# Three steps of an attention pipeline change places: the scaling of probabilities, the compressed branch's exponentials, and the compressed branch's PSUM banks

## The chip, the cores and the metric

The kernel runs on one core of one Trainium2 chip. The metric is device time in microseconds (us) of one execution. The kernel before has a median of 1531.22 us over 3 runs (1530.23 to 1532.88).

The engines are called as the profile calls them: PE (TensorE, matrix products), PEld (its weight loads), DVE (VectorE), ACT (ScalarE), POOL (GpSimd) and SP (SyncE, which issues DMAs). Each works through its own list of instructions in order and waits on semaphores for the others.

## The reference, cut to what matters

One decoder layer over 512 positions of width 2048, all in float32. A normalised input is projected to everything that the layer needs. Mixer A is the attention that this change touches; mixer B is a gated spatial mixer; both are projected up, merged by gates, projected out and added to the residual.

```python
h = rms_norm(x, norm_g[l])
proj = h @ w_in[l]
q, kv, g_logits, z_a, uv, z_b, merge_logits = jnp.split(proj, SPLIT_IDX, axis=-1)
o_a = nsa_attention(q, k_c, v_c, k_s, v_s, k_w, v_w, g_logits, ...) * jax.nn.silu(z_a)
o_b = spatial_gating(uv, ln_v_g[l], ln_v_b[l], sgu_w[l], sgu_b[l]) * jax.nn.silu(z_b)
merged = g_a * (o_a @ w_up_a[l]) + g_b * (o_b @ w_up_b[l])
x = x + merged @ w_out[l]
x = x + jax.nn.sigmoid(x @ w_ple_gate[l]) * (p[l] @ w_ple[l])
return rms_norm(x, final_g)
```

The attention has 16 heads in 4 groups of 4, and three branches with keys and values of their own: compressed (31 pooled keys), selected (blocks chosen by the compressed scores) and window. Each branch is a causal softmax with a linear position penalty per head, times a sigmoid gate:

```python
p_c = jax.nn.softmax(sc, axis=-1) * vc_mask
o_c = jnp.einsum('bgrqn,bngd->bqgrd', p_c.astype(vc.dtype), vc)
p_s = jax.nn.softmax(ss..., axis=-1)
p_w = jax.nn.softmax(sw, axis=-1)
o = gate_0 * o_c + gate_1 * o_s + gate_2 * o_w
```

With 512 positions there are 8 blocks and room for 16, so the selected branch takes every causal block, and the window of 512 takes every causal key. Both are therefore full causal attention, with different keys and values.

## The kernel before, in words

**The products.** Each large product is built from three matmuls in a fast float32 form: operands are cut into a high part (cast on ACT, `high`, line 162) and the remainder (subtraction on DVE, `low`, line 168), and high·high, high·low and low·high are added up in PSUM. A generator `gemm()` yields after each small step of these products, and `fill(n)` takes n steps. For the projections `q` and `za` a step is three matmuls of 128x512 (lines 451 to 453). So weight products can be put between any two other pieces of work on PE. `flush()` runs the list `deferred`, in which a step leaves what it wants issued later, often the `low` of a cast just made.

**The attention stage.** It is a pipeline over 48 slots. A head pair `ft` (8 of them, two per group) has six slots, `j` from 0 to 5: a tile `i` of 128 queries, with one of the two long branches or both. Slots 0 and 1 are the two branches of tile 3 (512 keys each), slots 2 and 3 those of tile 2 (384 keys), slot 4 has both branches of tile 1 (256 keys each), slot 5 both of tile 0 (128 each). The loop of line 1592 goes over slots `s` and 3 more steps, builds a list `events`, and runs it. That list is the order of the work, since every engine's list is filled in the order of the calls:

- `front(s)` first transposes the probabilities of slot s-2 on PE (`transpose_probs`, line 1440, tile `ps_t`; the casts to `pth` follow on ACT, the remainders `ptl` are deferred to DVE), then calls `finish`, which also runs `flush()`, then computes the scores of slot s on PE (`scores`, line 1383, tile `ps_s`) and on DVE adds the position penalty and takes the row's extreme in one instruction per row block (line 1389, tiles `prob` and `st`).
- `weigh(s-1)` takes the reciprocal of the sums (line 1409) and scales the probabilities of the slot before by it and by the gate (line 1414), on DVE.
- `exponentials(s)` runs the exponentials of slot s on ACT (line 1398), with their sums.
- `values(s-3, ...)` multiplies the transposed probabilities with the values on PE (lines 1472 and 1473, tile `ps_o`); at the end of a tile `fold` adds up on ACT and DVE (lines 1486 to 1491).
- The compressed branch runs once per group, spread over slots: `cmp_scores` (two halves in the last slot of an odd `ft`, line 1510), `cmp_softmax` (even `ft`, slot 1: transposes on PE, copy on ACT, then `shift` deferred to DVE, lines 1538 to 1540, which itself defers `exps` to ACT, line 1535), `cmp_weigh` (slot 3, DVE and POOL), `cmp_transpose` (slot 4, lines 1558 and 1560) and `cmp_values` (slot 5 of an even `ft`, slot 3 of an odd one, line 1570).

Between events the loop fills in weight products, so many steps per slot that the projections `q` and `za` are spread over the whole stage. An event in `off_pe` has no PE work: it is neither preceded by `flush()` nor followed by a fill.

**The banks.** PSUM is handed out in kinds of two banks each. Kind `s` serves `ps_s` (both banks, one per head) and `ps_c`, the compressed branch's bank, in turn; kind `t` serves `ps_t` (both banks). Whoever wants a bank again waits until its last reader is done: for `ps_s` that is line 1389 on DVE, for `ps_c` a copy on ACT, for `ps_t` the `ptl` remainders on DVE.

Of the kernel before, what the change touches and what calls it, by code (L numbers as in the profile page):

```python
# [16 lines left out]
AF = mybir.ActivationFunctionType  # L17
# [62 lines left out]
def kernel(ctx: ExitStack, tc: tile.TileContext, x, p, norm_g, w_in,  # L80
                      pe_k, w1_k, w2_k, pe_v, w1_v, w2_v, ln_g, ln_b, sgu_w, sgu_b,
                      w_up_a, w_up_b, w_out, w_ple, w_ple_gate, final_g, out):
    nc = tc.nc
# [68 lines left out]
    deferred = []  # L152
# [347 lines left out]
    def finish(name):  # L500
        while name not in done:
            next(run)
        flush()
# [729 lines left out]
    with tc.tile_pool(name="cmp", bufs=1) as cmp:  # L1233
# [76 lines left out]
        c = cmp.tile([P, 1], F32, name="hid_c")  # L1310
# [137 lines left out]
    def front(s):  # L1448
        if 2 <= s <= n_slots + 1:
            transpose_probs(s - 2)  # L1450
        if s < n_slots:
            ft, i, br = slots[s]
            finish(f"q{ft}")
            if i == 3 and br[0] == 0 and ft:
                fill(1)
                lent.append(1)
            scores(s)
# [67 lines left out]
    def cmp_softmax(g):  # L1525
# [7 lines left out]
        def exps():  # L1533
            for r in range(4):
                nc.scalar.activation(c[:, :, r], c[:, :, r], AF.Exp, scale=SLOPE[4 * g + r])

        def shift():
# [4 lines left out]
            deferred.append(exps)  # L1542
        deferred.append(shift)
        pct_t["c"] = (c, st)

# [29 lines left out]
    off_pe = (cmp_keys, cmp_weigh, weigh, exponentials)  # L1575
# [18 lines left out]
    for s in range(n + 3):  # L1594
# [5 lines left out]
        if s < n:  # L1600
            ft, j = slots[s][0], s % 6
        if s < n + 2:
            events.append((front, s))
        if 1 <= s <= n:
            events.append((weigh, s - 1))
        if s < n and ft % 2 == 0 and j == 3:
            events.append((cmp_weigh, ft // 2))
        vq = [(values, s - 3, bi) for bi in range(len(blocks(s - 3)))] if s >= 3 else []
        more = s < n and ft % 2 == 1 and ft < 7 and j == 5
        if more:  # L1610
            events.append((cmp_scores, (ft + 1) // 2, 0))
        if s < n:
            events.append((exponentials, s))
        events += vq[:1]
        if more:
            events.append((cmp_scores, (ft + 1) // 2, 1))
        if s < n:
            if ft % 2 == 1 and ft < 7 and j == 3:
                events.append((cmp_keys, (ft + 1) // 2))
            if ft % 2 == 0 and (ft > 0 and j == 1 or j == 4):  # L1620
                events.append(({1: cmp_softmax, 4: cmp_transpose}[j], ft // 2))
# [4 lines left out]
        if s < n and j == 5 - 2 * (ft % 2):  # L1626
            events.append((cmp_values, ft))
        events += vq[1:]
        share = per_period / max(1, sum(e[0] not in off_pe for e in events))
# [604 lines left out]
```

## Time and profile before

| what | value |
|---|---|
| median of 3 runs | 1531.22 us (1530.23 to 1532.88) |
| the profiled execution's own time | 1532.3 us |
| its span, first to last instruction | 1530.6 us |
| mean granted TensorE clock | 0.996 |
| PE busy | 1500.9 us, 98% |
| PEld busy | 1228.2 us, 80% |
| DVE busy | 1241.4 us, 81% |
| ACT busy | 867.1 us, 57% |
| POOL busy | 394.0 us, 26% |

The attention stage lies between about 200 and 490 us of the span. In the profile an arrow in an instruction, `out<-in`, names what it writes and reads; in a wait, `A <- B`, it names who waited for whom. A row of the waits ends with the total, the number of times and the longest. A row of the timeline has start, duration, engine, line, operation, tiles, shapes, a count of merged instructions, and in brackets the idle time of the engine before it with what ended that. Matmuls overlap in their pipeline, so their shown durations are longer than the distance between their starts, and idle time of PE counts only from the shown end.

### The profile page before, as it was taken

To read this page: it belongs to the slowest core of one execution; us is meant where nothing else is said; L and a number is where in the kernel's file an instruction comes from. 1 tells how busy PE (TensorE), PEld (TensorE's weight loads), DVE (VectorE), ACT (ScalarE), POOL (GpSimd) and SP (SyncE) were. 2 spreads that over 40 slices of the span, in tenths; PEclk is the share of its full clock that TensorE was granted. 3 is DMA by queue.
4 is the path that set the end of the run, shared out by engine and by line. 5 is a ranking of instruction groups with operands and counts; after the bars stand their busy time and mean duration, and the time that the engine had idled before them with its cause. 6 is when DMAs were issued, how large, how long until landed. Compare 5 with 4: busy or idle time off the path is not lost.

```text
span 1530.6 us, 21378 instructions
## 1 busy us (share of the span) xinstructions
PE 1500.9 (98%) x7565; PEld 1228.2 (80%) x7565; DVE 1241.4 (81%) x1882; ACT 867.1 (57%) x1501; POOL 394.0 (26%) x632
## 2 busy tenths in 40 slices
PE   9999999999989999999999999999999999999997
PEld 8988876776767888888888888888888888888886
DVE  7887878888887788978897979787877986678877
ACT  7554566666665555545555565555556565544556
POOL 1331044333442232342334333431010002100000
PEclk9999999999999999999999999999999999999999
DMA  9788579779793986887686977897697869955555
GB/s 331 195 255 288 143 163 209 157 180 233 158 243 120 304 253 183 268 197 258 145 249 196 243 207 234 249 331 255 227 336 254 237 200 321 312 178 176 182 206 192
DMA packets 183707, 346.88 MB, mean 227 GB/s; under 512 B 15016, under 2 KB 75056, under 8 KB 180400
## 3 DMA queue, kind: packets, MB, share of 16 engines
q0 software_dynamic: 70544, 172.61, 41.2%
q1 hardware_dynamic: 112912, 172.64, 35.2%
q8 instruction: 59, 0.97, 0.3%
q14 instruction: 48, 0.39, 0.1%
q10 hardware_dynamic: 144, 0.26, 0.0%
HBM read 283.08 MB, written 109.58 MB: 257 GB/s over the span
## 4 chain that ended last, share of the span: by engine, by line
PE 90%; DVE 5%; ACT 3%; issue 1%; DMA 0%; DVEq 0%; POOL 0%; ACTq 0%; POOLq 0%
PE ps_m L424 7%; PE ps_m L425 7%; PE ps_m L426 7%; PE ps_wo L425 3%; PE ps_wo L426 3%; PE ps_wo L424 3%; PE ps_kv L424 2%; PE ps_ub L426 2%; PE ps_kv L426 2%; PE ps_pg L426 2%; PE ps_pg L424 2%; PE ps_ua L424 2%; PE ps_zb L426 2%; PE ps_zb L425 2%; PE ps_vn L426 2%; PE ps_ub L424 2%
## 5 line engine op out<-in xcount | busy, mean ns | idle before, releaser
L168 DVE TENSOR_TENSOR ls<-b,hs 128x1024 fp32r<-128x1024 f32 x224 | 273.8, 1223 | 113.8 <-ACT hs L162 112.7
L162 ACT CAST hs<-b 128x1024 fp32r<-128x1024 f32 x224 | 235.5, 1053 | 205.7 <-PE ps_m L426 51.2
L162 ACT CAST hs<-raw 128x1024 fp32r<-128x1024 f32 x130 | 137.0, 1054 | 134.9 <-issue 33.7
L168 DVE TENSOR_TENSOR ls<-raw,hs 128x1024 fp32r<-128x1024 f32 x130 | 158.9, 1223 | 46.2 <-ACT hs L162 45.9
L424 PE MATMUL ps_m<-hs,act_h 128*128 128x512 f32 x256 | 100.1, 391 | 0.0
L425 PE MATMUL ps_m<-ls,act_h 128*128 128x512 f32 x256 | 99.7, 389 | 0.0
L426 PE MATMUL ps_m<-hs,act_l 128*128 128x512 f32 x256 | 99.6, 389 | 0.0
L304 DVE TENSOR_TENSOR b<-raw,b 128x1024 f32<-128x1024 f32 x76 | 92.6, 1219 | 3.2 <-DMA raw<-in_w_in_dram 3.1
L168 DVE TENSOR_TENSOR lo<-raw,hi 128x512 fp32r<-128x512 f32 (+1 forms) x120 | 79.1, 662 | 16.2 <-ACT hi L162 7.2
L1398 ACT ACTIVATE prob<-prob,st 128x512 f32<-128x512 f32 (+3 forms) x128 | 70.7, 554 | 33.6 <-DVE st L1389 33.6
L162 ACT CAST hi<-raw 128x512 fp32r<-128x512 f32 (+1 forms) x120 | 70.2, 595 | 33.1 <-PE ps_pg L466 10.5
L304 DVE TENSOR_TENSOR b<-b,b 128x1024 f32<-128x1024 f32 x72 | 87.8, 1219 | 0.0
L168 DVE TENSOR_TENSOR ptl<-ps_t,pth 128x512 fp32r<-128x512 f32 (+2 forms) x96 | 53.3, 597 | 36.3 <-ACT pth L162 35.6
L162 ACT CAST pth<-ps_t 128x512 fp32r<-128x512 f32 (+2 forms) x96 | 44.7, 517 | 39.5 <-PE ps_t L1440 39.1
L382 POOL COPY pad_r<-pad_r 128x1 f32<-128x1 f32 x39 | 30.6, 785 | 116.8 <-ACT pad_r L381 116.8
L1389 DVE CUSTOM_DVE_ANT_0 prob<-ps_s,b 128x512 f32<-128x512 f32 (+3 forms) x128 | 56.0, 484 | 2.9 <-PE ps_s L1383 2.9
L426 PEld LDWEIGHTS ps_m<-hs,act_l 128*128 128x128 f32 x256 | 48.1, 188 | 10.1
L424 PEld LDWEIGHTS ps_m<-hs,act_h 128*128 128x128 f32 x256 | 48.1, 188 | 9.8
L425 PEld LDWEIGHTS ps_m<-ls,act_h 128*128 128x128 f32 x256 | 48.1, 188 | 9.8
L1414 DVE TENSOR_SCALAR prob<-prob,st,gates 128x512 f32<-128x512 f32 (+3 forms) x128 | 53.8, 473 | 1.8
L451 PE MATMUL ps_q<-act_h,hi 128*128 128x512 f32 x128 | 54.5, 426 | 0.0
L451 PE MATMUL ps_za<-act_h,hi 128*128 128x512 f32 x128 | 53.7, 420 | 0.0
(747 smaller groups left out, 4479.5 us busy)
## 6 DMA issues: line engine op xcount, KB each, us to landing
raw<-in_w_in_dram SPq DMA_DIRECT2D x112, 512.0 KB, 5.6
b<-in_w_in_dram SPq DMA_DIRECT2D x58, 512.0 KB, 6.9
o<-in_w_out_dram POOLq DMA_DIRECT2D x48, 512.0 KB, 7.7
t<-in_w_up_b_dram POOLq DMA_DIRECT2D x24, 512.0 KB, 9.7
raw<-in_w_ple_gate_dram SPq DMA_DIRECT2D x24, 512.0 KB, 3.8
b<-o SPq DMA_DIRECT2D x18, 512.0 KB, 5.9
o<-o POOLq DMA_DIRECT2D x16, 512.0 KB, 5.9
act_l<-gate POOLq DMA_DIRECT2D x8, 1024.0 KB, 13.0
```

Of the source, the lines that this page charges most:

```text
L162: nc.scalar.copy(hi, src)
L168: nc.vector.tensor_tensor(out=lo, in0=src, in1=hi.bitcast(F32), op=ALU.subtract)
L304: nc.vector.tensor_tensor(out=b[o], in0=b[x], in1=b[y], op=ALU.subtract)
L382: nc.gpsimd.tensor_copy(steps[:, 16 + i:17 + i], steps[:, i:i + 1])
L424: nc.tensor.matmul(o, ah, wh, start=st, stop=False, skip_group_check=go)
L425: nc.tensor.matmul(o, ah, wl, start=False, stop=False, skip_group_check=go)
L426: nc.tensor.matmul(o, al, wh, start=False, stop=sp, skip_group_check=go)
L451: nc.tensor.matmul(ps, hi[:, j], ah, start=st, stop=False)
L1389: nc.vector.tensor_tensor_reduce(out=pt[:, j * n:j * n + n], in0=o[:, j], in1=b0[:, 512 - n:], scale=-SLOPE[h], scalar=3.0e38, op0=ALU.add ...
L1398: nc.scalar.activation(sl, sl, AF.Exp, bias=st[:, 0, j, hh:hh + 1], scale=-1.0, accum_out=st[:, 1, j, hh:hh + 1])
L1414: nc.vector.tensor_scalar(out=sl, in0=sl, scalar1=st[:, 1, j, hh:hh + 1], scalar2=gates[:, i, gate:gate + 1], op0=ALU.mult, op1=ALU.mult)
```

## The change

Three things change places; no instruction is added or taken away, and shapes stay as they are.

1. `weigh(s-1)` becomes the first event of slot s, ahead of `front(s)`. In `front(s)` the call of `finish`, with its `flush()`, comes before the transposes. The `ptl` remainders are therefore issued at the next flush, behind the scores' DVE instructions.
2. The compressed exponentials leave the deferred list and become an event of their own, `cmp_exps`, after `exponentials` in slot 2 of an even `ft`.
3. The compressed steps that take a PSUM bank of kind `s` (`cmp_scores`, `cmp_softmax`, `cmp_transpose`, `cmp_values`) move towards the end of the slot: the first `cmp_scores` behind the first `values`, the rest behind the last.

```diff
     def front(s):
+        if s < n_slots:
+            ft, i, br = slots[s]
+            finish(f"q{ft}")
         if 2 <= s <= n_slots + 1:
             transpose_probs(s - 2)
         if s < n_slots:
-            ft, i, br = slots[s]
-            finish(f"q{ft}")
             if i == 3 and br[0] == 0 and ft:
                 fill(1)
                 lent.append(1)
...
-        def exps():
-            for r in range(4):
-                nc.scalar.activation(c[:, :, r], c[:, :, r], AF.Exp, scale=SLOPE[4 * g + r])
-
         def shift():
...
-            deferred.append(exps)
         deferred.append(shift)
         pct_t["c"] = (c, st)
+
+    def cmp_exps(g):
+        c, _ = pct_t["c"]
+        for r in range(4):
+            nc.scalar.activation(c[:, :, r], c[:, :, r], AF.Exp, scale=SLOPE[4 * g + r])
...
-    off_pe = (cmp_keys, cmp_weigh, weigh, exponentials)
+    off_pe = (cmp_keys, cmp_exps, cmp_weigh, weigh, exponentials)
...
+        if 1 <= s <= n:
+            events.append((weigh, s - 1))
         if s < n + 2:
             events.append((front, s))
-        if 1 <= s <= n:
-            events.append((weigh, s - 1))
-        if s < n and ft % 2 == 0 and j == 3:
-            events.append((cmp_weigh, ft // 2))
+        if s < n:
+            if ft % 2 == 0 and j == 3:
+                events.append((cmp_weigh, ft // 2))
+            events.append((exponentials, s))
+            if ft % 2 == 0 and j == 2:
+                events.append((cmp_exps, ft // 2))
         vq = [(values, s - 3, bi) for bi in range(len(blocks(s - 3)))] if s >= 3 else []
         more = s < n and ft % 2 == 1 and ft < 7 and j == 5
+        events += vq[:1]
         if more:
             events.append((cmp_scores, (ft + 1) // 2, 0))
-        if s < n:
-            events.append((exponentials, s))
-        events += vq[:1]
-        if more:
-            events.append((cmp_scores, (ft + 1) // 2, 1))
-        if s < n:
-            if ft % 2 == 1 and ft < 7 and j == 3:
-                events.append((cmp_keys, (ft + 1) // 2))
-            if ft % 2 == 0 and (ft > 0 and j == 1 or j == 4):
-                events.append(({1: cmp_softmax, 4: cmp_transpose}[j], ft // 2))
+        if s < n and ft % 2 == 1 and ft < 7 and j == 3:
+            events.append((cmp_keys, (ft + 1) // 2))
...
-        if s < n and j == 5 - 2 * (ft % 2):
-            events.append((cmp_values, ft))
         events += vq[1:]
+        if more:
+            events.append((cmp_scores, (ft + 1) // 2, 1))
+        if s < n:
+            if ft % 2 == 0 and (ft > 0 and j == 1 or j == 4):
+                events.append(({1: cmp_softmax, 4: cmp_transpose}[j], ft // 2))
+            if j == 5 - 2 * (ft % 2):
+                events.append((cmp_values, ft))
```

The order of DVE's list shows the first and second part. The place is the third slot of head pair 2 (slot 2, tile 2 of one branch), the slot behind the first `cmp_softmax` of the loop. Before, `ptl_3113` are the remainders of the transposes at this slot's start, `prob_3127` and `prob_3129` this slot's scores, `prob_3044` and `prob_3046` the probabilities of the slot before:

```order
L1538 TENSOR_TENSOR b11_2898<-b11_2898,o32_582 128x512
L1539 TENSOR_REDUCE cst_3075<-b11_2898 128x16
L1540 TENSOR_TENSOR b11_2898<-b11_2898,cst_3075 128x512
L168 TENSOR_TENSOR ptl_3113<-ps_t_3094,pth_3112 128x512
L168 TENSOR_TENSOR ptl_3113<-ps_t_3095,pth_3112 128x512
L1389 ISA prob_3127,st_3118<-ps_s_3119,b0_2019 128x384
L1389 ISA st_3118 128x1
L1389 ISA prob_3129,st_3118<-ps_s_3120,b0_2019 128x384
L1389 ISA st_3118 128x1
L168 TENSOR_TENSOR lo_3136<-raw_2676,hi_3061 128x512
L1409 RECIPROCAL st_3035<-st_3035 128x2
L1414 TENSOR_SCALAR prob_3044<-prob_3044,st_3035,gates_578 128x512
```

Now, with `prob_3045` and `prob_3047` for the slot before, `prob_3124` and `prob_3126` for this slot's scores and `ptl_3112` for the remainders:

```order
L1409 RECIPROCAL st_3036<-st_3036 128x2
L1414 TENSOR_SCALAR prob_3045<-prob_3045,st_3036,gates_578 128x512
L1414 TENSOR_SCALAR prob_3047<-prob_3047,st_3036,gates_578 128x512
L1535 TENSOR_TENSOR b11_2906<-b11_2906,o32_582 128x512
L1536 TENSOR_REDUCE cst_3082<-b11_2906 128x16
L1537 TENSOR_TENSOR b11_2906<-b11_2906,cst_3082 128x512
L1389 ISA prob_3124,st_3115<-ps_s_3116,b0_2019 128x384
L1389 ISA st_3115 128x1
L1389 ISA prob_3126,st_3115<-ps_s_3117,b0_2019 128x384
L1389 ISA st_3115 128x1
L168 TENSOR_TENSOR ptl_3112<-ps_t_3093,pth_3111 128x512
L168 TENSOR_TENSOR ptl_3112<-ps_t_3094,pth_3111 128x512
```

The scaling of the slot before has moved from the end of the slot's list to its head, and the two `ptl` remainders from ahead of the scores' instructions to behind them.

The order of PE's list shows the third part at a `cmp_transpose`, slot 4 of the same head pair; `ps_c` is the compressed bank, `ps_t` and `ps_s` open the next slot. Before:

```order
L1558 MATMUL ps_c<-ident,b_2898 128x128 x4
L1472 MATMUL ps_o<-pth,vt 128x256
L1473 MATMUL ps_o<-ptl,vt 128x256
L1472 MATMUL ps_o<-pth,vt 128x256
L1473 MATMUL ps_o<-ptl,vt 128x256
L451 MATMUL ps_q_3224<-act_h_90,hi 128x512
L452 MATMUL ps_q_3224<-act_l_91,hi 128x512
L453 MATMUL ps_q_3224<-act_h_90,lo 128x512
L1440 MATMUL ps_t<-ident,prob 128x64 x12
L1383 MATMUL ps_s<-ob_h,b_2300 128x256 x4
```

Now:

```order
L1473 MATMUL ps_o<-pth,vt 128x256
L1474 MATMUL ps_o<-ptl,vt 128x256
L451 MATMUL ps_q_3224<-act_h_90,hi 128x512
L452 MATMUL ps_q_3224<-act_l_91,hi 128x512
L453 MATMUL ps_q_3224<-act_h_90,lo 128x512
L1559 MATMUL ps_c<-ident,b_2906 128x128 x4
L1440 MATMUL ps_t<-ident,prob 128x64 x12
L1383 MATMUL ps_s<-ob_h,b_2303 128x256 x4
```

The four transposes into `ps_c` now stand directly ahead of the next slot's transposes and scores; four value products and three weight products used to lie between. Elsewhere on PE the steps keep their places: the weight products stand at the same places in every slot that has no compressed step.

## The prediction

> **What bounds the kernel now.** I read the page's first part, then the busy times of three stretches, then the waits of the middle one, then the timeline at the longest of them.
>
> ```profile
> PE 1500.9 (98%) x7565; PEld 1228.2 (80%) x7565; DVE 1241.4 (81%) x1882; ACT 867.1 (57%) x1501; POOL 394.0 (26%) x632
> 0.00:200.00 200.00, 198.50 (x1014) 169.94 (x1015) 160.79 (x247) 115.90 (x214) 48.75 (x107) 1.00 0.78 237
> 200.00:490.00 290.00, 272.10 (x1928) 205.29 (x1928) 237.10 (x662) 186.32 (x496) 105.72 (x151) 0.99 0.79 187
> 490.00:1530.60 1040.60, 1030.31 (x4626) 852.93 (x4624) 843.50 (x974) 564.88 (x792) 239.55 (x375) 1.00 0.76 236
> ```
>
> The columns of the stretches are PE, PEld, DVE, ACT, POOL, granted clock, DMA. PE is the bound nearly everywhere. Of its 29.7 us of idle time, 17.9 lie in the attention stage (290.00 less 272.10), which is a fifth of the span. That is where the change works. So the question is what PE waits for there.
>
> The waits of that stretch, those that bear on PE and on the two engines that feed it:
>
> ```profile
> ACT pth L162 <- PE ps_t L1440: 39.1, 38, 2.5
> DVE ptl L168 <- ACT pth L162: 35.6, 32, 1.7
> ACT prob L1398 <- DVE st L1389: 33.6, 33, 2.1
> PE ps_t L1440 <- DVE prob L1414: 11.1, 15, 2.1
> ACT b L1535 <- DVE b L1540: 6.8, 4, 2.2
> PEld ps_t L1440 <- DVE prob L1414: 5.9, 17, 0.8
> PE ps_c L1570 <- DVE st L1389: 3.2, 4, 1.0
> PE ps_c L1510 <- DVE st L1389: 2.6, 3, 0.9
> ```
>
> PE waits in two places: the transposes wait for the scaling of the probabilities, and the compressed banks wait until DVE has read the scores out of the bank that they share. Behind that stands a ring on the other engines: DVE idles 35.6 us for the casts `pth`, with the scores' instructions queued behind, and ACT in turn idles 33.6 us for those.
>
> One full turn, from the third slot of head pair 2:
>
> ```profile
> 280.40 0.69 DVE L1538 TENSOR_TENSOR b<-b,o 128x512 f32<-128x512 f32 x1
> 280.76 0.71 PE L1440 MATMUL ps_t<-ident,prob 64*128 64x64 f32 x16
> 281.28 0.60 PE L1383 MATMUL ps_s<-ob_h,b 64*128 64x384 f32 x4
> 281.72 0.34 PE L1383 MATMUL ps_s<-ob_l,b 64*128 64x384 f32 x2
> 281.84 0.69 DVE L1540 TENSOR_TENSOR b<-b,cst 128x512 f32<-128x512 f32 x1
> 282.57 0.91 ACT L1535 ACTIVATE b<-b 128x128 f32<-128x128 f32 x4 [2.20 <-DVE b L1540]
> 283.39 1.05 ACT L162 CAST pth<-ps_t 128x512 fp32r<-128x512 f32 x2
> 283.99 1.29 DVE L168 TENSOR_TENSOR ptl<-ps_t,pth 128x512 fp32r<-128x512 f32 x2 [1.45 <-ACT pth L162]
> 285.19 0.55 DVE L1389 CUSTOM_DVE_ANT_0 prob<-ps_s,b 128x384 f32<-128x384 f32 x1
> 286.94 1.00 DVE L1414 TENSOR_SCALAR prob<-prob,st,gates 128x512 f32<-128x512 f32 x2
> 287.63 1.17 PE L1440 MATMUL ps_t<-ident,prob 64*128 64x64 f32 x16 [2.12 <-DVE prob L1414]
> ```
>
> The transposes are done by 281.5, but their cast starts at 283.39, since the compressed exponentials stand ahead of it on ACT and wait for DVE. DVE then waits for the cast, and only behind `ptl` and the scores' instructions comes the scaling that the next transposes need. They come 2.12 us late, and the group takes 1.17 us instead of 0.71, since its second head is scaled later still.
>
> **The transposes' wait goes.** Scaled at the head of the slot, the probabilities are ready a whole slot before their transposes; one slot is 290.00 / 51 = 5.7 us. What this frees is more than the idle time, because shown ends of matmuls run over the next start:
>
> ```profile
> 226.47 0.39 PE L451 MATMUL ps_q<-act_h,hi 128*128 128x512 f32 x1
> 226.70 0.40 PE L452 MATMUL ps_q<-act_l,hi 128*128 128x512 f32 x1
> ```
>
> Starts lie 0.23 apart where the shown length is 0.39, so each stall costs 0.16 more than its row says: 11.1 + 15 x 0.16 = 13.5 us. The 5.9 us of PEld are mostly the second heads, of which some are already among the 15; all of them would make 19.4. I take 16, near the middle, since the rows don't tell the shared ones apart.
>
> **The compressed banks' waits go**, since by a slot's end the scores have long been read: 3.2 + 2.6 + 7 x 0.16 = 6.9 us. DVE also reads them earlier, no longer behind `ptl`.
>
> **The clock.** Two stretches show half the granted clock (the column before the last two):
>
> ```profile
> 288.30:291.71 3.41, 3.41 (x24) 2.68 (x21) 2.68 (x9) 1.30 (x3) 2.05 (x3) 0.50 0.54 154
> 359.98:363.39 3.41, 3.41 (x11) 2.83 (x10) 3.37 (x10) 2.64 (x7) 0.08 (x1) 0.50 1.04 393
> ```
>
> The first begins right behind the 2.12 us wait above, and I read the second as the same thing one group later. Half speed costs 2 x 3.41 x 0.5 = 3.4 us. I take it as gone with the waits. [...]
>
> Gross: 16 + 6.9 + 3.4 = 26.3 us, between 23.8 and 29.7 by the bounds of the first term.
>
> **What is late next.** Three things can make PE wait afresh.
>
> First, the scores need both banks of kind `s`, and the compressed bank now fills just ahead of them. Before, there is one case of it:
>
> ```profile
> 227.32 0.63 PE L1558 MATMUL ps_c<-ident,b 128*128 128x128 f32 x4
> 228.85 0.60 ACT L162 CAST hi<-raw 128x512 fp32r<-128x512 f32 x1
> 229.06 0.58 PE L1440 MATMUL ps_t<-ident,prob 64*128 64x64 f32 x12
> 229.36 0.58 ACT L1560 COPY pc<-ps_c 128x512 f32<-128x512 f32 x1
> 229.45 0.36 PE L1383 MATMUL ps_s<-ob_h,b 64*128 64x256 f32 x1
> 229.99 0.50 PE L1383 MATMUL ps_s<-ob_h,b 64*128 64x256 f32 x3 [0.18 <-ACT pc L1560]
> ```
>
> The second head's score started 0.54 after the first instead of about 0.1. In the new order the four transposes into `ps_c` take some 0.4 us and end right ahead of the 12 others; the copy can start about 0.65 after their first (the first row's 0.63) and takes 0.58, while the scores come at about 0.85. So the second head waits some 0.45 us with ACT free, and 0.9 if a weight cast of 0.60 is in front: 1.8 to 3.6 us over the four groups; I take 2.5. Behind `cmp_values`, `cmp_softmax` and `cmp_scores` one step of weight products (3 x 0.23) and 16 transposes, or more, cover the copy: nothing. The first `cmp_scores` keeps only one step and four value products between itself and the scores: 0.3 us each, three times, 1 us.
>
> Second, `ptl` now follows the scores on DVE, and the transposes of the next slot want its banks. Group means of DVE and ACT for this:
>
> ```profile
> L168 DVE TENSOR_TENSOR ptl<-ps_t,pth 128x512 fp32r<-128x512 f32 x48 | 30.9, 686 | 21.0 <-ACT pth L162 20.9
> L1389 DVE CUSTOM_DVE_ANT_0 prob<-ps_s,b 128x512 f32<-128x512 f32 x32 | 20.7, 684 | 2.9 <-PE ps_s L1383 2.9
> L1414 DVE TENSOR_SCALAR prob<-prob,st,gates 128x512 f32<-128x512 f32 x32 | 17.2, 579 | 0.6
> L1398 ACT ACTIVATE prob<-prob,st 128x512 f32<-128x512 f32 x32 | 22.8, 716 | 10.5 <-DVE st L1389 10.5
> ```
>
> Counted from the transposes' start: scores ready at about 1.35 (280.76 to 282.06 in the turn above), read by DVE in 2 x 0.68 to about 2.8, `ptl` 2 x 0.69 to 4.2. Against a slot of 5.2 (5.7 less what the waits took) 1.0 us is left. In the slot behind `cmp_softmax` the three instructions of `shift`, each 0.69 like L1540 above, go ahead: copy done at 0.2 (1.23 behind the first transpose into `ps_c`, which comes 1.0 ahead), `shift` to 2.35, scores (2 x 0.55) to 3.45, `ptl` to 4.8. That leaves 0.4, and whatever else is late on DVE comes through. I put 1 us on each of the three such slots.
>
> Third, DVE is busy 237.1 us, and the stage is to shrink to some 270: 88%. Its idle time for `pth` is filled by the scores' instructions, but it will run late in places; 0.5 us more.
>
> New waits: 2.5 + 1 + 3 + 0.5 = 7 us. The compressed exponentials cost the same 0.91 us on ACT as before; in their own step they hold up no cast, since the slot's casts are ahead of them. No DMA, SP or POOL instruction moves past another queue's work, and from 490 us on PE has 1 us idle in 100, so what is won reaches the end.
>
> Net 26.3 - 7 = 19.3. Against the profiled execution's 1532.3 that is 1513.0; its time lies 1.1 above the median of the runs, 1531.2, from which it is 1511.9. I forecast 1512. The own range of this case, with bounds 23.8 and 29.7 and new waits of 3 to 12, is 1504 to 1519.
>
> **The rivals.**
>
> *Half is given back* (1519 to 1526). Every transpose group now hangs on `ptl`, at 4.2 of 5.2 us, where scaling hung before. If DVE runs a slot's fifth late as a rule, each of 48 groups loses about 0.2 us more, and the clock drops stay: 9.6 + 3.4 off the 19.3 leaves 6, so 1525; with the clock mended 1522. For it: DVE's 82% in the stage is the highest after PE. Against: its 35.6 us of waiting for casts go, and they were part of what made it late.
>
> *Slower* (about 1545). Scaling now stands ahead of the scores' instructions and needs the exponentials of the slot before. DVE takes its list in order, so while `weigh(s-1)` waits for ACT, the reading of scores, `ptl` and the weights' remainders wait too, and ACT's next exponentials with them: a ring of scores, exponentials and scaling that must fit in a slot. Its parts for 512 keys are 0.76 for the first head's scores, 2 x 0.716 + 0.19 of exponentials and 0.16 + 2 x 0.58 of scaling, together 3.7 us. ACT's weight cast and two `pth` casts (0.60 + 1.05) make it 5.4 if both fell inside. It decides from 5.7 us on: with a second weight cast of 0.60 in between it would be 6.0, and 48 slots at 0.3 more than now would be 14 us, 1545. Against: the casts come out of the transposes, half a microsecond ahead of the scores, and can run while DVE reads these.
>
> *No change* (1530). PE gets through the stage earlier, but what follows is not ready, a weight load above all, and it waits there instead. For it: the DMA share is 0.76 to 0.79 throughout. Against: no wait of PE for a DMA stands among those of the stage.
>
> **How the numbers follow.** Forecast 0.65, half given back 0.20, no change 0.07, slower 0.08. About 0.2%, 3.1 us, is what a measurement of this kernel can tell from no change. Faster by more: the first two, 0.85; within: 0.07; slower: 0.08. The range takes the first two cases, with half a microsecond below for the bounds: 1503.5 to 1526.
>
> **What would show it.** Right: the wait of the transposes for L1414 is gone from PE and PEld, those of `ps_c` for L1389 too; DVE's wait for `pth` falls well below 35.6; no stretch of the stage has half clock; PE's idle time between 200 and 490 less the gain falls from 17.9 to under 8. The new waits would stand as `ps_s` for ACT's `pc`, in four places, and `ps_t` for `ptl`, behind `cmp_softmax`. Wrong: DVE's L1414 waiting for ACT's L1398 by tens of microseconds, `ps_t` waiting for `ptl` in most slots, or PE idle after the stage where it wasn't.

## The result and the profile after

| what | before | after |
|---|---|---|
| median of 4 runs | 1531.81 us (1530.23 to 1532.88) | 1508.69 us (1506.67 to 1510.0) |
| ratio, with its 95% interval | | 0.9849 [0.9832, 0.9866] |
| the profiled execution's own time | 1532.3 us | 1508.67 us |
| its span | 1530.6 us | 1507.0 us |
| mean granted TensorE clock | 0.996 | 0.998 |

The kernel is 23.1 us faster; 19.3 were forecast. First the busy times on the page, then of three stretches, for after. The stage now lies between 195 and 470 us; columns as before: PE, PEld, DVE, ACT, POOL, granted clock, DMA.

```profile
PE 1492.6 (99%) x7565; PEld 1226.0 (81%) x7565; DVE 1242.1 (82%) x1882; ACT 867.6 (58%) x1501; POOL 395.1 (26%) x632
0.00:195.00 195.00, 193.52 (x992) 166.57 (x993) 155.84 (x238) 112.60 (x208) 44.38 (x98) 1.00 0.78 240
195.00:470.00 275.00, 273.41 (x1975) 211.06 (x1974) 245.54 (x676) 193.31 (x508) 111.52 (x165) 1.00 0.84 199
470.00:1507.00 1037.00, 1025.67 (x4602) 848.39 (x4600) 840.70 (x970) 561.72 (x787) 239.17 (x371) 1.00 0.76 237
```

PE's idle time in the stage fell from 17.9 to 1.6 us (275.00 less 273.41), and the granted clock there is 1.00. Outside the stage PE now idles 12.8 us (1507.0 less 1492.6, less 1.6) where it was 11.8 (29.7 less 17.9): one microsecond came back later. The waits of after in the stage, those that answer to the rows shown of before and those that are new:

```profile
ACT pth L162 <- PE ps_t L1440: 28.7, 37, 1.4
ACT prob L1398 <- DVE st L1389: 22.7, 24, 3.7
DVE prob L1389 <- PE ps_s L1383: 12.2, 14, 1.8
DVE st L1409 <- ACT prob L1398: 2.7, 5, 0.8
PEld ps_t L1440 <- DVE ptl L168: 1.4, 3, 0.7
PEld ps_s L1383 <- ACT pc L1561: 1.3, 4, 0.6
PEld ps_t L1440 <- DVE prob L1414: 0.7, 2, 0.4
PE ps_t L1440 <- DVE ptl L168: 0.6, 2, 0.4
PE ps_c L1559 <- DVE st L1389: 0.4, 1, 0.4
PE ps_s L1383 <- ACT pc L1561: 0.4, 1, 0.4
```

The 11.1 us of PE behind L1414 are gone, and of PEld's 5.9 are left 0.7. The banks' 5.8 us behind L1389 are down to a single wait of 0.4. DVE has no row of waiting for `pth` any more (35.6 before). It waits instead for the scores out of PE, 12.2 us. The same turn as before, the third slot of head pair 2, in the timeline of after:

```profile
275.49 0.71 PE L1440 MATMUL ps_t<-ident,prob 64*128 64x64 f32 x16
276.45 0.35 PE L1383 MATMUL ps_s<-ob_l,b 64*128 64x384 f32 x2
277.74 0.55 DVE L1389 CUSTOM_DVE_ANT_0 prob<-ps_s,b 128x384 f32<-128x384 f32 x1
278.69 1.28 DVE L168 TENSOR_TENSOR ptl<-ps_t,pth 128x512 fp32r<-128x512 f32 x2
279.55 0.90 ACT L1545 ACTIVATE b<-b 128x128 f32<-128x128 f32 x4
280.16 0.71 PE L1440 MATMUL ps_t<-ident,prob 64*128 64x64 f32 x16
280.69 0.87 DVE L1414 TENSOR_SCALAR prob<-prob,st,gates 128x384 f32<-128x384 f32 x2
```

The scores end at 276.80 and DVE reads them 0.94 us later; before it was 285.19 less 282.06, or 3.1. The compressed exponentials run on ACT behind the slot's other work. The transposes at 280.16 need no fresh scaling: what runs at 280.69 is for the slot after them. Their group takes 0.71 instead of 1.17, and from one group to the next it is 4.67 us (280.16 less 275.49).

### The profile page after: what moved, and what is told of

Same layout as the page of the kernel before. It is cut to its first block, busy times and chain, and to the rows that moved or that the text cites. A ratio compares the mean times of both kernels' runs of the same rounds, so it can differ in the third digit from the quotient of the medians.

```text
span 1507.0 us, 21330 instructions
## 1 busy us (share of the span) xinstructions
PE 1492.6 (99%) x7565; PEld 1226.0 (81%) x7565; DVE 1242.1 (82%) x1882; ACT 867.6 (58%) x1501; POOL 395.1 (26%) x632
## 4 chain that ended last, share of the span: by engine, by line
PE 92%; DVE 3%; DMA 3%; ACT 1%; issue 1%; POOL 0%; DVEq 0%; ACTq 0%; POOLq 0%
PE ps_m L425 6%; PE ps_m L426 6%; PE ps_m L424 6%; PE ps_wo L425 3%; PE ps_wo L426 3%; PE ps_wo L424 3%; PE ps_q L451 2%; PE ps_s L1383 2%; PE ps_za L451 2%; PE ps_q L452 2%; PE ps_q L453 2%; PE ps_kv L425 2%; PE ps_ub L425 2%; PE ps_kv L426 2%; PE ps_ub L424 2%; PE ps_pg L425 2%
## 5 line engine op out<-in xcount | busy, mean ns | idle before, releaser
L1389 DVE CUSTOM_DVE_ANT_0 prob<-ps_s,b 128x512 f32<-128x512 f32 (+3 forms) x128 | 56.3, 486 | 13.1 <-PE ps_s L1383 12.2
L1414 DVE TENSOR_SCALAR prob<-prob,st,gates 128x512 f32<-128x512 f32 (+3 forms) x128 | 55.8, 492 | 1.8
```

The costliest lines, as they stand in the source:

```text
L1389: nc.vector.tensor_tensor_reduce(out=pt[:, j * n:j * n + n], in0=o[:, j], in1=b0[:, 512 - n:], scale=-SLOPE[h], scalar=3.0e38, op0=ALU.add ...
L1414: nc.vector.tensor_scalar(out=sl, in0=sl, scalar1=st[:, 1, j, hh:hh + 1], scalar2=gates[:, i, gate:gate + 1], op0=ALU.mult, op1=ALU.mult)
```

## The experiments

The change has two halves in its first part. I call W the scaling (`weigh`) put ahead of `front`, F the `finish` with its flush put ahead of the transposes, which sends `ptl` behind the scores on DVE, X the compressed exponentials as a step of their own, and B the compressed banks at the slot's end. Every time below is a median, with its ratio to the kernel before, which ran beside it, and the 95% interval of that ratio. PE's idle time is given for 200 to 490 us, "the 290". Line numbers of the compressed steps differ by one or two between kernels. Theory in brief: PE's waits come from the order of DVE's and ACT's lists, and the gain is these waits gone. The rivals were that one part alone carries it, that the ring through the exponentials costs part of it, and that the gain comes by way of the clock.

### The parts put in alone

**W and F together**, from the kernel before:

```diff
-        if 2 <= s <= n_slots + 1:
-            transpose_probs(s - 2)
         if s < n_slots:
             ft, i, br = slots[s]
             finish(f"q{ft}")
+        if 2 <= s <= n_slots + 1:
+            transpose_probs(s - 2)
+        if s < n_slots:
...
-        if s < n + 2:
-            events.append((front, s))
         if 1 <= s <= n:
             events.append((weigh, s - 1))
+        if s < n + 2:
+            events.append((front, s))
```

> The first part of the change alone: scaling ahead of the slot's front, and the flush ahead of the transposes; compressed exponentials and banks as before. Theory A (each part takes away the waits that name it): the transposes' wait for scaling goes, 16 us, and both half-clock stretches, 3.4 us; of the compressed banks' 6.9 us some 2 go since DVE reads the scores earlier. 1510 to 1514, with 4 to 5 us still shown on ps_c. Rival B (the compressed exponentials, ahead of the casts on ACT, cause the long waits and the clock drops): three waits of about 2 us stay, now on ptl, with their clock drops; no more than 12 us faster, 1520 or later.

Measured: 1517.82 us, 0.9911 [0.9897, 0.9924]. Between the two theories. The waits of the stage:

```profile
PE ps_c L1571 <- DVE st L1389: 6.2, 4, 1.6
PE ps_c L1559 <- DVE st L1389: 1.6, 1, 1.6
```

The transposes' wait for the scaling is gone without X and B (0.7 us of PEld left), the clock is 1.00, and of the 9.9 us that PE still idles in the 290 the compressed banks are 7.8, more than the 4 to 5 that I had put on them.

**X alone**: the list entry goes, and `cmp_exps` becomes an event.

```diff
-            deferred.append(exps)
...
+            if ft % 2 == 0 and j == 2:
+                events.append((cmp_exps, ft // 2))
```

> The second part alone: the compressed exponentials as an event of their own, behind the slot's exponentials. Theory A: the three waits of about 2 us behind the softmax step shrink by the 0.9 us of the exponentials and by ACT's wait for them, so some 3 us are won, and 3.4 more if the clock no longer drops: 1525 to 1529. Rival B: nearly all of these three waits and the clock drops go, 10 us: 1521.

Measured: 1524.80 us, 0.9956 [0.9943, 0.9968], at the edge of theory A. PE's wait for L1414 fell from 11.1 to 6.7 us, its longest from 2.1 to 0.8, and no stretch of half clock is left (3.4 us). The two together, 4.4 and 3.4, cover the 6.6 us that it gains. The casts of `pth` no longer queue behind the exponentials.

**B alone**: the four compressed steps move, as in the change's diff.

```diff
-        if more:
-            events.append((cmp_scores, (ft + 1) // 2, 0))
...
-            if ft % 2 == 0 and (ft > 0 and j == 1 or j == 4):
-                events.append(({1: cmp_softmax, 4: cmp_transpose}[j], ft // 2))
...
-        if s < n and j == 5 - 2 * (ft % 2):
-            events.append((cmp_values, ft))
         events += vq[1:]
+        if more:
+            events.append((cmp_scores, (ft + 1) // 2, 1))
+        if s < n:
+            if ft % 2 == 0 and (ft > 0 and j == 1 or j == 4):
+                events.append(({1: cmp_softmax, 4: cmp_transpose}[j], ft // 2))
+            if j == 5 - 2 * (ft % 2):
+                events.append((cmp_values, ft))
```

> The third part alone: the compressed steps that take a bank move to the slot's end. Theory A: the waits of ps_c for the scores' DVE instructions go, 6.9 us, and the second head's scores wait for the copy behind the compressed transposes, 2 to 4 us; the rest stays: 3 to 5 us faster, 1527 to 1529. Rival C (a bank wait only moves the stall, since the scaling is late in any case): the transposes' wait grows by what the banks gave, and the time stays within 2 us of 1531.8.

Measured: 1523.76 us, 0.9948 [0.9934, 0.9961]: 7.7 us, above what was expected. `ps_c` waits 0.4 us in all. The surplus is a side effect: the compressed softmax begins later in its slot, so ACT's wait for its DVE steps fell from 6.8 to 1.1 us, PE's wait for L1414 from 11.1 to 9.1 (its longest from 2.1 to 1.0), and the half clock went too. So these 7.7 us are not the banks' alone.

**F alone**: the first hunk of W and F above, without the second.

> Half of the first part: only the flush moves ahead of the transposes, so that the remainders ptl stand behind the scores' DVE instructions; the scaling stays behind the slot's front. Theory A: DVE's 35.6 us of idle time for the casts fall below 15, the scaling comes about 1 us earlier, and most of the transposes' 10 us of first waits go; the three long ones fall to about 1 us. 8 to 14 us faster, 1518 to 1524. Rival D (only the place of the scaling counts): DVE's idle time falls, but the scaling is the last thing in its slot either way, and no more than 4 us are won.

Measured: 1526.76 us, 0.9969 [0.9956, 0.9981]: 4.7 us, near rival D's 4 and far from theory A's 8. The waits:

```profile
DVE prob L1389 <- PE ps_s L1383: 36.3, 41, 2.0
PE ps_t L1440 <- DVE prob L1414: 12.4, 23, 0.9
DVE ptl L168 <- ACT pth L162: 2.2, 3, 1.2
```

DVE's idle time only changed its name: 35.6 us for casts became 36.3 for scores, and the scaling behind them is as late as it was (12.4 against 11.1). The gain is the `ps_c` waits, which are gone since DVE reads the scores before `ptl`, and one of the two stretches of half clock, 1.7 us. So "DVE's waiting for `pth` falls", which I had listed as a sign that the forecast is right, is no evidence by itself.

### The parts left out of the whole

**W alone**, the second hunk without the first, is the other half of the same test:

> The other half of the first part alone: scaling ahead of the slot's front, the flush (and so ptl ahead of the scores' DVE instructions) as before. The first part as a whole gave 13.6 us, its flush alone 4.7. Theory A (the place of the scaling carries the gain): the transposes' wait for L1414 and the half clock go, the ps_c waits grow, since scaling and ptl now both stand ahead of the scores' instructions: 1516 to 1521, 10 to 15 us faster than before. Rival E (scaling in front without the flush only moves the wait): DVE idles for the casts with the scores queued behind, ps_c waits reach 10 us or more, and no more than 8 us are won: 1523 or later.

Measured: 1538.56 us, 1.0045 [1.0032, 1.0059], **slower by 7.3 us**; neither theory had that size. Waits of its stage:

```profile
ACT prob L1398 <- DVE st L1389: 57.5, 36, 5.2
DVE st L1409 <- ACT prob L1398: 11.0, 28, 0.8
PE ps_c L1570 <- DVE st L1389: 10.9, 8, 2.6
PE ps_c L1558 <- DVE st L1389: 6.1, 3, 3.4
```

and its timeline at the same place as the two turns above:

```profile
283.60 0.34 PE L1383 MATMUL ps_s<-ob_l,b 64*128 64x384 f32 x2
284.97 1.00 DVE L1414 TENSOR_SCALAR prob<-prob,st,gates 128x512 f32<-128x512 f32 x2
286.31 1.29 DVE L168 TENSOR_TENSOR ptl<-ps_t,pth 128x512 fp32r<-128x512 f32 x2 [0.33 <-ACT pth L162]
287.51 0.55 DVE L1389 CUSTOM_DVE_ANT_0 prob<-ps_s,b 128x384 f32<-128x384 f32 x1
288.60 0.29 PEld L1383 LDWEIGHTS ps_s<-ob_h,b 64*128 64x128 f32 x3 [0.29 <-DVE st L1389]
```

The transposes have what they need, but now the scores come last on DVE, behind the scaling and behind `ptl`, which itself waits for the casts. They end at 283.94 and are read at 287.51, 3.6 us later; the next scores and the compressed banks (17.0 us in these two rows of `ps_c`; L1570 had 3.2 before, L1558 no row) wait for the bank, and ACT for the scores. PE idles 23.5 us in the 290 instead of 17.9, and two stretches of half clock stand in it.

**All but W**, the change with `weigh` put back behind `front`:

```diff
-        if 1 <= s <= n:
-            events.append((weigh, s - 1))
         if s < n + 2:
             events.append((front, s))
+        if 1 <= s <= n:
+            events.append((weigh, s - 1))
```

> The whole change except that the scaling stays behind the slot's front. Theory A: the transposes still wait for L1414, 10 us and more in some 20 waits, with none near 2 us and no half clock; ps_c waits are gone: 1517 to 1521. Rival F (with exponentials and banks moved, nothing makes the scaling late any more): 1512 or earlier.

Measured: 1531.68 us, 1.0002 [0.9993, 1.0011]. **No gain at all** from F, X and B together, though each alone gives 4.7 to 7.7 us. Its waits:

```profile
DVE prob L1389 <- PE ps_s L1383: 36.0, 40, 2.0
PE ps_t L1440 <- DVE prob L1414: 13.5, 24, 1.0
PEld ps_t L1440 <- DVE prob L1414: 6.8, 21, 0.8
```

The banks no longer wait, and the transposes wait more than ever (13.5 and 6.8, against 11.1 and 5.9); beside them stand 2.1 us of `ps_t` waiting for `ptl` and a stretch of half clock at 415.0, where none was expected. I read this as PE getting sooner to the point where it must wait for the scaling, in a slot that is as long as DVE's list from scores to scaling; no run tests that reading by itself. That the transposes' wait would stay was expected; that it would take back all of the rest was not.

**All but F**, the change with `finish` back behind the transposes:

```diff
     def front(s):
-        if s < n_slots:
-            ft, i, br = slots[s]
-            finish(f"q{ft}")
         if 2 <= s <= n_slots + 1:
             transpose_probs(s - 2)
         if s < n_slots:
+            ft, i, br = slots[s]
+            finish(f"q{ft}")
```

> The whole change without the earlier flush: ptl stays ahead of the scores' DVE instructions. Theory A (scaling in front pushes the scores' instructions back, and only the flush pulls them forward again; what is late then is whatever wants the banks of the scores): ps_c waits remain even at the slot's end, some 8 us of the 26 that scaling alone showed: 1514 to 1520. Rival J (banks at the slot's end cover any lateness of the scores): 1511 or earlier.

Measured: 1521.09 us, 0.994 [0.9926, 0.9953], a microsecond above the range that I gave. Late scores again, and the wait shows mostly where the compressed copy gives its bank to the scores:

```profile
ACT prob L1398 <- DVE st L1389: 52.8, 36, 5.2
DVE st L1409 <- ACT prob L1398: 14.2, 35, 0.8
PE ps_s L1383 <- ACT pc L1560: 4.8, 4, 1.4
PE ps_c L1558 <- DVE st L1389: 2.7, 3, 2.3
```

PE idles 8.2 us of the 290, and half clock begins three times, the last time for twice the usual length (431.4 to 438.3). All stretches together are 13.65 us long and cost 6.8. Against 1.6 us of idle time and no half clock in the whole, that is 13.4 us. The gain is 9.6 us and falls 13.5 short of the whole's 23.1, so these two account for it.

**All but X**, the exponentials back on the deferred list:

```diff
+            deferred.append(exps)
...
-            if ft % 2 == 0 and j == 2:
-                events.append((cmp_exps, ft // 2))
```

> The whole change with the compressed exponentials left on the deferred list, so that they may stand ahead of the casts pth on ACT. Theory A (with the scaling in front nothing on PE waits for that cast but through ptl, which has a microsecond to spare): 1 to 3 us slower than the whole change, 1509.5 to 1512. Rival B (the exponentials ahead of the cast make the long waits): three waits of 1.5 us and more of ps_t for ptl, half clock again: 1515 or later.

Measured: 1512.61 us, 0.9885 [0.9871, 0.9898]. It gains 18.0 us; X is worth some 5 within the whole. ACT waits 7.5 us for the compressed softmax's DVE steps with the casts behind it. PE idles 3.5 us of the 290, 1.9 more than in the whole, and one stretch of half clock, of double length again (422.8 to 429.6), costs 3.4: together 5.3. Within the whole, then, most of what X gives is the clock.

Side by side, us below (+) or above (-) the kernel before:

| part | alone | left out, the rest gains | worth within the whole |
|---|---|---|---|
| W | -7.3 | -0.4 | 23.5 |
| F | 4.7 | 9.6 | 13.5 |
| X | 6.6 | 18.0 | 5.1 |
| B (left out with X) | 7.7 | 13.6 (W and F) | 9.5 with X |

Each gain is against the kernel before that ran beside it; the last column is the whole's 23.1 less the one beside it. The intervals of the ratios are 3 to 5 us wide, so a difference of 5 is only just told from nothing. B was not left out by itself, but all but X is W, F and B: there B adds 4.4 us to the 13.6 of W and F, less than its 7.7 alone. The parts alone sum to 11.7. The whole is twice that, so the parts are not terms of a sum.

### The new waits

**The compressed bank a step earlier**: from the changed kernel, `cmp_transpose` goes ahead of the slot's last values, so that its copy is done before the scores want the bank.

```diff
+        if s < n and ft % 2 == 0 and j == 4:
+            events.append((cmp_transpose, ft // 2))
         events += vq[1:]
...
-            if ft % 2 == 0 and (ft > 0 and j == 1 or j == 4):
-                events.append(({1: cmp_softmax, 4: cmp_transpose}[j], ft // 2))
+            if ft % 2 == 0 and ft > 0 and j == 1:
+                events.append((cmp_softmax, ft // 2))
```

> The changed kernel, but the compressed transposes of slot 4 go back ahead of the slot's last value products, so that these lie between the bank and the next slot's scores. Theory A: the second head's scores no longer wait for the copy, four times 0.4 us, and the chain of three waits of the last group (0.60, 0.66 and 0.73 us) goes as well: 2 to 3.5 us faster than the changed kernel, 1505 to 1507. Rival G (the bank then waits for the scores' DVE instructions instead): within 1 us of 1508.7.

Measured: 1509.74 us, 0.9857 [0.9843, 0.987]: no better. The wait moved: `ps_s` for `pc` is down to 0.4 and 0.2 us (PEld and PE), but the banks wait for the scores again, 2.7 us of PE at `cmp_values` and 1.6 at `cmp_transpose`, where the changed kernel has 0.4 in all.

**More work on DVE**: from the changed kernel, one addition of 128x256 per slot behind the scaling, which nothing reads.

```diff
+    idle = att.tile([P, 256], F32, name="idle")
...
+        nc.vector.tensor_tensor(out=idle, in0=b0[:, :256], in1=b0[:, 256:], op=ALU.add)
```

> The changed kernel with one more DVE instruction per slot, an addition of 128x256 that nothing reads, behind the scaling and ahead of the scores' instructions: about 0.4 us in 48 slots, 20 us of DVE's list. DVE idles some 29 us of the stage. Theory A (PE is the bound and DVE has room): no more than 6 us slower than 1508.7. Rival H (scores, exponentials and scaling have become a ring that sets the slot): most of the 20 us come through, 1520 or later.

Measured: 1512.43 us, 0.988 [0.9867, 0.9894]: 18.9 us of gain are left of 23.1. DVE is busy 267.0 us of the 290. Its idle time before the scores fell to 3.9 us, and `ps_t` waits 2.4 us for `ptl` (0.6 without the additions). The 48 additions take 0.42 us each, 20 in all, and about 4 us of them reach the time, which bears out theory A: DVE had slack, which came out of its waits for scores first, and little reached PE.

### What a better order gives

**The compressed weights away from the scaling**: in the changed kernel `cmp_weigh` sends two multiplications to POOL, and the scaling comes right behind on DVE. Here it goes between `weigh` and `front` in slot 3, so that they run before the next scaling.

```diff
         if 1 <= s <= n:
             events.append((weigh, s - 1))
+        if s < n and ft % 2 == 0 and j == 3:
+            events.append((cmp_weigh, ft // 2))
         if s < n + 2:
             events.append((front, s))
         if s < n:
-            if ft % 2 == 0 and j == 3:
-                events.append((cmp_weigh, ft // 2))
```

> The changed kernel with the compressed weighing one place earlier, right behind the scaling at the head of slot 3, so that its two multiplications on POOL no longer run beside the next slot's scaling on DVE. There one scaling of 128x384 takes 2.33 us in the changed kernel's trace and two others 1.01 and 1.02, where the mean is 0.52. Theory K (DVE's scaling is held while POOL's multiplication runs, and the chain of waits of the last group comes from it): no scaling over 0.96 us beside those multiplications, that chain gone, 1.5 to 3 us faster than 1508.7. Rival L (the long one has another cause, or the multiplications hold the scores' instructions instead): no faster.

Measured: 1506.89 us, 0.9843 [0.983, 0.9857]. The traces show the scaling no longer held (the last section has the lines). By time it gains 23.8 us where the change gains 23.1; the two intervals overlap, so a gain over the changed kernel isn't shown by the times. PE's idle time in the 290 falls from 1.6 to 1.0 us.

**Both**: that, and the one step of weight products that the loop puts ahead of `cmp_transpose` goes behind it instead, as cover for the copy.

```diff
-                ahead = at + 1 < len(events) and events[at + 1][0] is cmp_transpose
+                ahead = 0
```

> The same, and one step of weight products that stood ahead of the compressed transposes of slot 4 stands behind them, so that the scores' second head comes 0.7 us later and finds the copy done. Theory A: the waits of ps_s for ACT's pc, 1.3 us on PEld, go as well: 2.5 to 4.5 us faster than 1508.7, 1504 to 1506. Rival G (the bank, now 0.7 us earlier, waits for the scores' DVE instructions instead, as it did when it was moved ahead of the values): no faster than the kernel without this step.

Measured: 1505.59 us, 0.9836 [0.9822, 0.9849]; 25.1 us below the kernel before, where the changed kernel is 23.1 below. No wait of `ps_s` for `pc` is left in its stage, and `ps_t` for `ptl` is 0.9 us. It is the fastest version that ran; its interval and that of the change still overlap a little.

## Why the prediction was right, step by step

**The place.** Right: 16.3 of the 23.6 us between the two profiled executions are PE's idle time in the stage, 3.4 are the clock, 1.0 was lost behind the stage, and the remaining 4.9 are time in which PE is shown busy: its busy time fell by 8.3 us (1500.9 less 1492.6) for the same 7565 instructions, of which the clock is 3.4. I put the 4.9 down to what rows hide where shown ends run over the next start (22 waits at 0.16 were 3.5 in the forecast).

**The transposes' wait.** Right, it is gone (0.7 us of PEld left). That it carries most is shown by leaving W out: 1531.68. But the prediction reached this by adding a wait's rows, 16 us, as if it could be had alone, and it can't: W alone costs 7.3 us. W and F together gave 13.6 us where this term and the clock made 19.4; B and X gave the other 9.5, where 6.9 and nothing were put on them. That the terms still add up to nearly the right time is in part luck. The three kinds of work on DVE in a slot are the scores' reading, `ptl` and the scaling, and each order makes one of them last. Before, and with F alone, it is the scaling, for which the next transposes wait. With W alone it is the scores, for which banks and exponentials wait. With both it is `ptl`, which is wanted only by the transposes of the next slot. The prediction named F's effect ("DVE also reads them earlier, no longer behind `ptl`") and gave it no price.

**The compressed banks.** Right that these waits go: 5.8 us of rows are down to 0.4. The size of 6.9 is neither shown nor refuted: B is worth 7.7 alone, but with the clock and the ACT queue's relief inside it, and 4.4 on top of W and F, where the banks waited 7.8.

**The clock.** The 3.4 us are gone, as forecast. But the drops were put down too simply to waits of some 2 us, as the last section shows, and X alone or B alone is enough to be rid of both stretches, without W. Leaving W, F or X out of the whole brings half clock back.

**The compressed exponentials.** Their own cost is unchanged (0.90 us), and they hold up no cast: right. The prediction gave the move no gain of its own; it is worth 6.6 us alone and some 5 within the whole, 3.4 of each by the clock.

**What is late next.** This is the mis-sized term: 7 us forecast. All rows of PE and PEld that wait for `pc` or `ptl` in the stage make 1.3 + 0.4 + 1.4 + 0.6 = 3.7 us. PE itself idles only 1.6 us there, and 1.0 us more came back behind the stage. That makes 2.6, and 26.3 less the 23.6 that came leaves 2.7. By its parts: the scores' second head does wait for `pc`, in four places as said. One of them, with the last group's:

```profile
291.71 0.29 PEld L1383 LDWEIGHTS ps_s<-ob_h,b 64*128 64x128 f32 x3 [0.24 <-ACT pc L1561]
420.45 0.29 PEld L1383 LDWEIGHTS ps_s<-ob_h,b 64*128 64x128 f32 x3 [0.63 <-ACT pc L1561]
```

They are 1.3 us where 2.5 was taken. In three of the four places the copy found ACT free, and PEld waits 0.2 us, half of the 0.45 that was reckoned for that case, with no idle time on PE behind it. Only in the last group does PE wait too, 0.4 us. The first `cmp_scores`, 1 us, shows no wait. The 3 us for the slots behind `cmp_softmax` did not come: in the turn above, which is such a slot, `ptl` ends at 279.97, 4.5 us behind its transposes where I had 4.8, and the next ones at 280.16 show no wait for it. Only 0.2 us were left, where I had 0.4; but a lateness that just fits costs nothing, and that "whatever else is late on DVE comes through" was a guess. The two PE waits for `ptl` stand in the last group, for a reason that the prediction passed over. It said that no POOL instruction moves past another queue's work; the scaling moved beside POOL's multiplications, as the last section shows.

**The rivals.** *Half given back* hung on `ptl` in every slot; it waits in at most five places. *Slower* had the right ring: with W and without F, DVE's scaling waits 11.0 to 14.2 us for the exponentials, ACT 53 to 58 us for the scores, and alone it is slower. In the changed kernel the scaling waits 2.7 us. The point from which it decides was wrong: not that the ring's parts sum to 5.7 us, the length of a slot, but whether `ptl` with its cast stands between the scaling and the scores. *No change* by a late weight load: no wait of PE for a DMA turned up.

## What to carry to other kernels

On an engine that takes its list in order, look at all the work of one period and ask who waits for each piece, and when; the piece to put last is the one whose reader comes last. Moving a late piece to the front alone can cost more than it wins, because another becomes the last one, so moves that fix such an order are tried together, and their gains are not added from rows of waits. Where an engine's idle time changes only the name of what it waits for, nothing has been won yet.

## What the runs showed of the hardware

**A scaling on DVE can be held up by a multiplication on POOL.** In the second and in the last group of the changed kernel's stage:

```profile
285.86 1.33 POOL L1552 TENSOR_TENSOR b<-b,cst 128x512 f32<-128x512 f32 x1 [0.94 <-DVE cst L1551]
286.40 1.56 DVE L1414 TENSOR_SCALAR prob<-prob,st,gates 128x384 f32<-128x384 f32 x2
287.27 0.47 POOL L1553 TENSOR_TENSOR b<-b,o 128x128 f32<-128x128 f32 x1
414.10 2.33 DVE L1414 TENSOR_SCALAR prob<-prob,st,gates 128x384 f32<-128x384 f32 x1
414.10 2.86 DVE L1414 TENSOR_SCALAR prob<-prob,st,gates 128x384 f32<-128x384 f32 x2
414.70 1.50 POOL L1552 TENSOR_TENSOR b<-b,cst 128x512 f32<-128x512 f32 x1
416.28 0.47 POOL L1553 TENSOR_TENSOR b<-b,o 128x128 f32<-128x128 f32 x1
417.34 0.51 ACT L1398 ACTIVATE prob<-prob,st 128x256 f32<-128x256 f32 x1 [3.69 <-DVE st L1389]
418.86 0.27 PE L1440 MATMUL ps_t<-ident,prob 64*128 64x64 f32 x1 [0.44 <-DVE ptl L168]
```

The two rows at 414.10 are the first scaling alone and the pair. The pair that took 0.87 us at 280.69 takes 1.56 and 2.86 here. It ends at 287.96 and 416.96, 0.22 and 0.21 behind POOL's second multiplication. The first scaling of the last group takes 2.33 us and ends at 416.43, 0.23 behind the first multiplication. So in these rows the end of a scaling hangs on the end of the multiplication beside it. In the last group the scores, the exponentials and `ptl` slip with it, down to four waits of PE between 417.79 and 420.46 (for `ps_c`, twice for `ptl`, and for `pc`). They make 1.5 us, nearly all of the 1.6 that PE still idles in the stage. The scaling's durations over the whole run (smallest, median and largest ns of one), in the changed kernel and with `cmp_weigh` moved:

```profile
L1414 DVE TENSOR_SCALAR prob<-prob,st,gates x128: 335/475/2326, 209.1 to 457.0; 128x512 f32<-128x512 f32 x32, 128x384 f32<-128x384 f32 x32, 128x256 f32<-128x256 f32 x32, 128x128 f32<-128x128 f32 x32
```

```profile
L1414 DVE TENSOR_SCALAR prob<-prob,st,gates x128: 334/476/954, 209.1 to 456.7; 128x512 f32<-128x512 f32 x32, 128x384 f32<-128x384 f32 x32, 128x256 f32<-128x256 f32 x32, 128x128 f32<-128x128 f32 x32
```

The longest falls from 2.33 to 0.95 us, much as it was before the change (0.94). One pair of 1.52 us is left, beside another POOL instruction (L697), and it ends 0.22 behind that. The ends agree: these scalings are done 0.21 to 0.23 us behind the POOL instruction beside them, whether that takes 0.47 or 1.50 us. A scaling was held with either of the two first: in the second group the multiplication begins 0.54 us ahead of it, in the last the scaling begins 0.60 us ahead of the multiplication's shown start. Spans on POOL are rough in the profile, and why a scaling is held is not shown by any run here.

**Half clock without an idle stretch.** The two stretches of half clock in the stage of the kernel before are 3.413 us long and begin 71.68 us apart, 21.0 times that length; the last one of its trace, at 1523.92, begins 362.0 such lengths behind the first. So I count lengths of 3.413 us from a drop and set each such stretch beside the one that follows. At half clock the products of 128x512 start 0.43 us apart (360.00 and 360.43) where it is 0.23 otherwise (226.47 and 226.70). The stretches just ahead of the two drops in the kernel before:

```profile
284.89:288.30 3.41, 1.20 (x15) 0.66 (x13) 3.37 (x10) 2.11 (x7) 0.00 (x0) 1.00 0.81 219
356.57:359.98 3.41, 1.75 (x23) 1.37 (x24) 2.73 (x9) 2.50 (x8) 0.65 (x1) 1.00 1.06 414
```

and with F alone, PE's columns only, the stretch ahead of the drop and the drop:

```profile
341.12:344.53 3.41, 2.23 (x18) 1.00 1.06 121
344.53:347.95 3.42, 3.42 (x13) 0.50 0.98 204
```

PE shows work in 1.20 to 2.23 of the 3.41 us, a third to two thirds, and the clock is halved right behind. The longest wait of PE in the three is 2.12, 1.89 and 0.89 us.

How much work shown on PE doesn't decide it alone. In the kernel before, this stretch, 40 lengths behind the first drop, has less than the 2.23 above, and the clock stays whole behind it. PE's columns only, this stretch and the one that follows:

```profile
424.83:428.25 3.42, 1.89 (x11) 1.00 1.08 338
428.25:431.66 3.41, 2.98 (x29) 1.00 1.03 313
```

Of the 2.23, transposes into `ps_t` are 0.83; the stretch with 1.89 has none. A wait of PE of 1.87 us, from 426.72 to 428.59, lies across the two rows, and no drop follows. What sets a drop off is not shown: no run varied it alone.

In this kernel, then, stretches whose longest wait was 0.89 to 2.12 us were followed by half clock. By my estimate a drop costs 1.7 us on top (half of 3.41), or 3.4 where it lasts two lengths, as it did without X.
